# A hybrid RG-LRU and chunked attention layer: gates one step further behind, a bias table of distances in DRAM, and rearranged background loads

## The chip, the core and the metric

One core of a Trainium2 chip runs the whole kernel in one launch. The metric is the device time in microseconds (us) of one execution; the profile is one further execution, taken with the hardware profiler.

## What is computed

One layer of a streaming encoder, for 2048 prompt tokens and 32 sample tokens. Cut to what matters here:

```python
z = rms_norm(x, norm_g) @ w_in                 # 1024 -> 6 x 512
xl, gl, q, k, v, ga = split(z)
xc = b + sum(full[:, k:k + T] * w[k] for k in range(4))      # causal conv of xl
r = sigmoid(block_diag(xc, wa) + ba); i = sigmoid(block_diag(xc, wx) + bx)
log_a = -8 * r * softplus(-lam); a = exp(log_a)
u = sqrt(-expm1(2 * log_a)) * (i * xc)
h = scan(h[t] = a[t] * h[t-1] + u[t])                        # RG-LRU
s = q @ k.T / 8 + table[clip(distance, -256, 256)]           # per head, 64 + 512 frames
att = softmax(s) @ v
mix = concat([h * silu(gl), att * silu(ga)]) @ w_out
y = x + mix, then + (p @ w_pe) * sigmoid(rms_norm(y) @ w_pg)
```

The sample reads cached keys and values of 512 frames besides its own. Outputs are y for prompt and sample, the newest keys and values, and the last convolution rows and LRU states.

## The kernel before

Every matrix product is made of fp16 halves: each operand is split into a high and a low part, and three matmuls (high by high, high by low, low by high) stand for one (`products`, L177 to 185). The parts need a power-of-two scale, which comes from a maximum over the whole tensor; `all_max` (L81 to 91) takes it across partitions with a diagonal, one small matmul into a PSUM bank of its own (`psm`) and a reduction.

The prompt is 16 tiles of 128 tokens. `load_x` and `prep_x` (L214 to 236) load a tile, normalise and split it and transpose it by DMA into xT. `proj(i, b)` (L268) makes 24 matmuls of 512 columns for tile i and one of the four attention blocks of w_in (q, k, v, gate), and the `post_*` functions spill the result to DRAM. The w_in blocks are loaded and split at the start (`load_w_in`, `prep_w_in`, L243 to 264), through staging tiles of eight slots.

The LRU works in 8 chunks of 256 tokens, four blocks g of 128 channels each. `l_proj` (L537) makes 48 matmuls into a `psx` bank, ACT copies both halves out (the gate half z as it is), the conv is one POOL and three DVE instructions, and `l_split` makes X. `l_gates` (L593) makes four matmuls of X into the only `psg` bank; ACT takes two sigmoids each of r and of i (`th`) from it, POOL multiplies by i. `l_tail` (L612) works on all four blocks together: Tanh, two Exp, Sqrt and the sigmoid of z on ACT, then the scans and a product. `l_halves` spills the result. `l_steps` (L653) hands these out, with the gates one block behind.

The main loop (c = 2 to 5, from L762) takes eight steps a chunk; each step makes one attention projection, parts of the LRU of the chunk before, and three steps of `background` (L350), a generator of side jobs: the cached keys' and values' bounds and halves, the bias of each of eight heads, and bounds and halves of the output weights. For the bias, a 511-column row of each head's table, stored in DRAM (`ext_d`, L695 to 699), is loaded skewed to 128 partitions (L418), scaled by POOL, widened by ACT, masked by two memsets and stored to `bias_d`; four loads bring it back at the start of the attention (L892). Chunks 6 and 7 run in a denser phase after the loop, then the attention and the output stage.

The tile framework orders each engine's instructions by a simulated timeline: an instruction that is ready may be placed far ahead of its place in the program, unless it stands under `issue_after`, and a tile's slot is taken when its first instruction is placed. DMAs of the kernel are issued from SP in order.

Of the kernel before, what the change touches and what calls it, by code (L numbers as in the profile page):

```python
# [13 lines left out]
OP = mybir.AluOpType  # L14
# [20 lines left out]
def hybrid_layer(  # L35
# [91 lines left out]
    bias_d = dp.tile([128, H, 640], F32, name="biasd")  # L127
# [75 lines left out]
    ps_g = pool("ps_g", bufs=1, space=PSUM, stack=esl)  # L203
    ps_m = pool("ps_m", bufs=1, space=PSUM, stack=esl)
# [146 lines left out]
    def background():  # L351
        def load(src):
            st = stg_tile()
            nc.sync.dma_start(st, src)
            return st
# [4 lines left out]
        def bound(src):  # L360
            m = sm.tile([128, 2], F32, tag="ckm", name="ckm")
            for j in range(2):
                with tc.issue_after(last_w.ins):
                    st = load(cache(src, j))
                yield
                absmax(m[:, j:j + 1], st)
            nc.vector.tensor_tensor(m[:, 0:1], m[:, 0:1], m[:, 1:2], op=OP.max)
            a = sm.tile([128, 1], F32, tag="cka", name="cka")
            for _ in range(4):
                yield  # L370
            all_max(a, m[:, 0:1], last_mm[0])
            return a

        m = yield from bound(cache_k)
        absmax(mgq, gk_b)
        nc.vector.scalar_tensor_tensor(m, mgq, 8.0, m, op0=OP.mult, op1=OP.max)
        floor2(mbS, m)
        nc.vector.reciprocal(sS, mbS)
        nc.vector.tensor_scalar(sS, sS, 2.0 ** 14, None, op0=OP.mult)
        nc.vector.tensor_scalar(gkS, gk_b, sS, None, op0=OP.mult)  # L380
        absmax(mgq, gq_b)
        floor2(mgq, mgq)
        nc.vector.tensor_scalar(ratS, mbS, 2.0 ** -28, iscP, op0=OP.mult, op1=OP.mult)
        nc.vector.tensor_tensor(ratS, ratS, mgq, op=OP.mult)
        nc.vector.reciprocal(mgq, mgq)
        nc.vector.tensor_scalar(gqS, gq_b, mgq, 0.5, op0=OP.mult, op1=OP.mult)
        for j in range(2):
            st = load(cache(cache_k, j))
            yield
            for d in range(2):  # L390
# [7 lines left out]
                yield  # L398
        m = yield from bound(cache_v)
        mbV, sV = c1("mbV"), c1("sV")  # L400
        nc.vector.tensor_copy(mbV, m)
        nc.vector.reciprocal(sV, mbV)
        nc.vector.tensor_scalar(sV, sV, 2.0 ** 14, None, op0=OP.mult)
        nc.vector.reciprocal(ratC, u_v)
        nc.vector.tensor_scalar(ratC, ratC, mbV, 2.0 ** -34, op0=OP.mult, op1=OP.mult)
        for j in range(2):
            st = load(cache(cache_v, j))
            yield
            for d in range(2):
                t = Tp("vTo", [128, 2, 512], F16, 2)  # L410
                split(t[:, 0], t[:, 1], st[:, d], sV)
                nc.sync.dma_start(kc_d[2 * j + d][:, 1], t.rearrange("p a b -> p (a b)"))
                yield


        for h in range(H):
            bq = stg_tile().rearrange("p a b -> p (a b)")[:, :384]
            nc.sync.dma_start(bq, bass.AP(tensor=ext_d.tensor, offset=ext_d.offset + 511 * h, ap=[[1, 128], [1, 384]]))  # L418
            yield
# [10 lines left out]

        jobs = [(u_out[n], None, 0, 1.0, block(w_out[0], wo_d[n], n)) for n in range(2)]
        jobs += [(u_pg[n], 1, PG, 2.0 ** -11, block(w_ple_gate[0], wg_d[n], n)) for n in range(2)]
        jobs.append((u_pe, None, 0, 0.5, [(w_ple_proj[0, :, n * 512:(n + 1) * 512], we_d[:, n], 0) for n in range(2)]))
        for u, gcol, gsrc, um, parts in jobs:
            a = sm.tile([128, 4], F32, tag="absT", name="absT")

            def get(src):
                return load(src.rearrange("(k p) n -> p k n", p=128))

            nxt = get(parts[0][0])  # L440
            for j in range(len(parts)):
                st = nxt
                nxt = get(parts[(j + 1) % len(parts)][0])
                yield
                junk = Tp("hlA", [128, D], BF16, 2)
                nc.scalar.activation(junk, st.rearrange("p a b -> p (a b)"), AF.Abs, accum_out=a[:, j:j + 1])
            for _ in range(4):
                yield
            ma = w_max(a[:, :len(parts)], last_mm[0])
            yield  # L450
            sg = w_factors(ma, gcol, gsrc, u, um)
            for j, (_, dst, k0) in enumerate(parts):
                st = nxt
                if j + 1 < len(parts):
                    nxt = get(parts[j + 1][0])
                yield
                for k in range(2):
                    hl = Tp("hlA", [128, 2, 512], F16, 2)
                    s = sg[:, k0 + k:k0 + k + 1] if gcol is not None else sg[:, 0:1]
                    split(hl[:, 0], hl[:, 1], st[:, k], s)  # L460
                    nc.sync.dma_start(dst[:, k], hl)
# [79 lines left out]
    def l_proj(c, g):  # L541
# [26 lines left out]
        nc.scalar.activation(z, pt[:, 1, :n], AF.Copy, scale=u_gl)  # L568
# [13 lines left out]
    def l_split(c, g):  # L582
        n = width(c)
        xc = C[c]["i4"][:, g, :n]
        X = TL("X", [128, 2, CW], F16, 3)
# [26 lines left out]
    def l_tail(c):  # L612
        n, t = width(c), C[c]
        r, u, th, z, sq = (t[k][:, :, :n] for k in ("r4", "i4", "th4", "sl4", "sq4"))
        nc.vector.tensor_tensor(r, r, bc4(cl, n), op=OP.mult)
        nc.scalar.activation(th, r, AF.Tanh, scale=-1.0)
        nc.scalar.activation(sq, r, AF.Exp, scale=2.0)
        nc.scalar.activation(r, r, AF.Exp)
        nc.vector.scalar_tensor_tensor(th, sq, 1.0, th, op0=OP.add, op1=OP.mult)
        nc.scalar.activation(th, th, AF.Sqrt)  # L620
        nc.scalar.activation(sq, z, AF.Sigmoid)
        nc.vector.tensor_tensor(th, th, u, op=OP.mult)
        nc.gpsimd.tensor_tensor(z, z, sq, op=OP.mult)
        for g in range(4):
            init = 0.0 if c == 0 else col[:, SLR + g:SLR + g + 1] if c == SAMPLE else hlast[g]
            h = t["i4"][:, g, :n]
            nc.vector.tensor_tensor_scan(h, t["r4"][:, g, :n], th[:, g], init, op0=OP.mult, op1=OP.add)  # L627
            if c != SAMPLE:
                hlast[g] = h[:, n - 1:n]
            if c in (SAMPLE, NCH - 1):  # L630
                o = (28 if c == SAMPLE else 12) + g
                nc.vector.tensor_copy(small[:, o:o + 1], h[:, n - 1:n])
        nc.vector.tensor_tensor(z, t["i4"][:, :, :n], z, op=OP.mult)
# [19 lines left out]
    def l_steps(c):  # L653

        for g in range(5):
# [3 lines left out]
            if g:  # L659
                l_gates(c, g - 1)  # L660
# [108 lines left out]
    for c in range(2, NCH - 2):  # L769
        steps = [(i, b) for i in (2 * c, 2 * c + 1) for b in (1, 0, 2, 3)]  # L770
        lp, ls = ls, l_steps(c - 1)
        for n, (i, b) in enumerate(steps):
# [6 lines left out]
            for _ in range(3):  # L779
                next(bg, None)  # L780
# [111 lines left out]
    for h in range(0, H, 2):  # L892
        nc.sync.dma_start(bias[:, h:h + 2], bias_d[:, h:h + 2])
# [8 lines left out]
    def s_bias(u):  # L902

        S = T("S", [128, 640], F32, 3, ch)
        for j in range(4):
            nc.sync.dma_start(S[j * NS:(j + 1) * NS, :512 + NS], bias_d[:NS, 2 * j + u, :512 + NS])
# [345 lines left out]
```

## Time and profile before

| | before |
|---|---|
| median of 3 runs | 1249.12 us (1247.4 to 1251.3) |
| the profiled execution, its own time | 1244.72 us |
| span of the profiled execution | 1243.0 us |
| mean granted clock of TensorE | 0.951 |
| DMA bytes moved | 215.36 MB |

PE is TensorE, PEld its weight loads, DVE VectorE, ACT ScalarE, POOL GpSimd, SP the engine that issues DMAs. Waits are given with what ended them: the engine and line that released the waiting instruction. Times in a timeline count from the start of the span. A clock of 1.00 is full speed.

### The profile page before, as it was taken

Reading aid. Unit: us, or ns where it says so; the run is one execution under the profiler, and the core shown is the slowest. Engines: PE = TensorE matmul, PEld = TensorE weight load, DVE = VectorE, ACT = ScalarE, POOL = GpSimd, SP = SyncE. Lnnn points to the kernel's source line nnn. Section 1 sums busy time; section 2 is a strip of 40 time slices with the busy share of each in tenths; the row PEclk is TensorE's granted clock in tenths of the full one; section 3 lists DMA queues with packets and bytes.
Section 4 is the critical chain, followed back from the end, with each engine's and each line's share of the span. In section 5 each row is a group of like instructions: output and inputs, shape, how many; then the busy total and the mean of one; then the engine's idle time right before and its main releaser. Section 6 shows DMA issues by size and latency. Waiting matters only on the chain.

```text
span 1243.0 us, 22344 instructions
## 1 busy us (share of the span) xinstructions
PE 1074.7 (86%) x8365; PEld 621.9 (50%) x8365; DVE 827.6 (67%) x1804; ACT 613.3 (49%) x1078; POOL 479.6 (39%) x543
## 2 busy tenths in 40 slices
PE   3799998868698879898895589999999999999895
PEld 1345664643454555575642345555555555555442
DVE  5897465635775867657646685677777767777544
ACT  6532656347355857265664344444444444444223
POOL 2885243544643547454421221322222222222211
PEclk9899999988899989898997789999999999999998
DMA  8795317567658468341597987899889999999830
GB/s 293 188 231 173 86 37 174 146 195 190 192 148 233 145 196 231 100 109 35 160 313 233 235 157 156 177 203 188 185 189 191 183 198 191 192 198 188 197 69 26
DMA packets 357068, 215.36 MB, mean 173 GB/s; under 512 B 296016, under 2 KB 299392, under 8 KB 356832
## 3 DMA queue, kind: packets, MB, share of 16 engines
q1 hardware_dynamic: 356528, 213.41, 71.4%
q8 instruction: 65, 1.06, 0.4%
q10 hardware_dynamic: 432, 0.54, 0.1%
q14 instruction: 43, 0.35, 0.1%
HBM read 97.30 MB, written 46.24 MB: 115 GB/s over the span
## 4 chain that ended last, share of the span: by engine, by line
PE 21%; DMA 10%; DVE 9%; issue 5%; ACT 4%; POOL 2%; SPq 1%; POOLq 0%; ACTq 0%; DVEq 0%
PE psu L184 8%; PE psg L184 7%; DMA PT<-Phl 6%; PE pss L933 2%; PE pso L988 2%; DVE Phl L966 2%; PE pse L184 2%; DVE S L944 2%; DMA hT<-hn 1%; ACT Phl L965 1%; POOL Phl L963 1%; ACT S L950 1%; DVE i L627 1%; DVE gt L1103 1%; DMA out_dram<-t 1%
## 5 line engine op out<-in xcount | busy, mean ns | idle before, releaser
L184 PE MATMUL psp<-wA,xT 128*128 128x512 f16 x1536 | 357.5, 391 | 26.6 <-DMA xT<-xn 7.9
L184 PEld LDWEIGHTS <-xT 128*128 128x128 f16 x1536 | 152.6, 100 | 225.7 <-issue 47.3
L950 ACT ACTIVATE S<-S,nb,s 128x640 f32<-128x640 f32 (+5 forms) x130 | 110.5, 850 | 214.6 <-DVE nb L947 208.7
L553 PE MATMUL psx<-xT,wl 128*128 128x256 f16 x1536 | 184.5, 281 | 0.5 <-DVE wl L164 0.5
L184 PE MATMUL psg<-g,hT 128*128 128x512 f16 x768 | 179.1, 381 | 2.9 <-DMA hT<-hn 2.8
L553 PEld LDWEIGHTS <-wl 128*128 128x128 f16 x1728 | 159.3, 100 | 33.0 <-issue 5.4
L966 DVE TENSOR_TENSOR Phl<-S,Phl 128x640 f16<-128x640 f32 (+4 forms) x126 | 97.9, 781 | 88.5 <-POOL Phl L963 51.5
L988 PE MATMUL pso<-kv,PT 128*128 128x64 f16 (+1 forms) x1704 | 116.6, 194 | 25.9 <-DMA PT<-Phl 13.2
L988 PEld LDWEIGHTS <-PT 128*128 128x128 f16 (+2 forms) x1800 | 109.4, 99 | 48.1 <-DMA PT<-Phl 16.9
L963 POOL TENSOR_SCALAR Phl<-S 128x640 f16<-128x640 f32 (+4 forms) x63 | 48.8, 774 | 205.0 <-ACT S L950 175.0
L933 PE MATMUL pss<-kv,qT 128*128 128x128 f16 (+2 forms) x1200 | 107.2, 222 | 10.4 <-DVE mx L944 8.3
L184 PEld LDWEIGHTS <-hT 128*128 128x128 f16 x768 | 71.2, 98 | 80.7 <-DMA hT<-hn 4.0
L933 PEld LDWEIGHTS <-qT 128*128 128x128 f16 (+1 forms) x1200 | 93.8, 99 | 33.3 <-issue 19.9
L944 DVE CUSTOM_DVE_ANT_0 S<-pss,bias 128x640 f32<-128x640 f32 (+4 forms) x128 | 92.9, 731 | 7.1 <-PE pss L933 7.0
L184 PE MATMUL psu<-o,AT 128*128 128x512 f16 x384 | 90.7, 387 | 1.1 <-DMA AT<-An 1.1
L184 PE MATMUL psu<-o,L 128*128 128x512 f16 x384 | 88.3, 379 | 0.0
L1104 POOL TENSOR_TENSOR gt<-gt,h 128x512 f32<-128x512 f32 x32 | 42.2, 1319 | 63.1 <-DVE gt L1103 54.0
L588 ACT ACTIVATE X<-i,sx 64x256 f16<-64x256 f32 x64 | 32.2, 504 | 67.5 <-DVE i L578 66.6
L578 DVE SCALAR_TENSOR_TENSOR i<-xl,col,i 128x256 f32<-128x256 f32 x96 | 52.1, 543 | 16.4 <-POOL i L575 14.7
L96 POOL TENSOR_TENSOR fh<-fh,pw 128x8 f32<-128x8 f32 (+1 forms) x34 | 61.1, 1797 | 2.0
L605 PE MATMUL psg<-X,gw 128*128 128x256 f16 (+1 forms) x72 | 18.4, 280 | 45.3 <-ACT th L609 29.8
L184 PEld LDWEIGHTS <-AT 128*128 128x128 f16 x384 | 36.3, 100 | 41.9 <-issue 3.3
(289 smaller groups left out, 1694.2 us busy)
## 6 DMA issues: line engine op xcount, KB each, us to landing
stw<-in_w_in_dram SPq DMA_DIRECT2D x20, 512.0 KB, 6.5
x<-in_x_prompt_dram SPq DMA_DIRECT2D x16, 512.0 KB, 4.5
stg<-in_w_out_dram SPq DMA_DIRECT2D x16, 512.0 KB, 5.7
stg<-in_w_ple_gate_dram SPq DMA_DIRECT2D x16, 512.0 KB, 4.9
qT<-qd SPq DMA_DIRECT2D x32, 256.0 KB, 5.4
kv<-kvd SPq DMA_DIRECT2D x16, 512.0 KB, 4.4
h<-in_x_prompt_dram SPq DMA_DIRECT2D x16, 512.0 KB, 4.6
out_dram<-gt SPq DMA_DIRECT2D x32, 256.0 KB, 2.4
```

Of the source, the lines that this page charges most:

```text
L96: nc.gpsimd.tensor_tensor(dst, dst, pw[:R, :n], op=OP.pow)
L184: m = nc.tensor.matmul(ps[:R], lhsT=l(a), rhs=r(e), start=first and j == 0, stop=last and j == 2)
L553: m = nc.tensor.matmul(o, lhsT=wl[j][:, k, a, g * 128:(g + 1) * 128], rhs=rhs, start=i == 0, stop=i == 23)
L578: nc.vector.scalar_tensor_tensor(xc, xl[:, k:k + n], col[:, CWT + 4 * k + g:CWT + 4 * k + g + 1], xc, op0=OP.mult, op1=OP.add)
L588: nc.scalar.activation(X[q, o, :n], xc[q], AF.Copy, scale=sx[q, g:g + 1])
L933: last_mm[0] = nc.tensor.matmul(ps[rw, c], lhsT=q[:, h % 2, a * 4 + h // 2, :R], rhs=k[:, h, :n], start=a == 0, stop=a == 1)
L944: nc.vector.tensor_tensor_reduce(out=S[:, c0:c0 + W], in0=ps[:, c0:c0 + W], in1=bias[:, h, 640 - W:], op0=OP.add, op1=OP.max, scale=1.0, s ...
L950: nc.scalar.activation(S[:, c0:c0 + W], S[:, c0:c0 + W], AF.Exp, bias=nb[:, j:j + 1], scale=scP, accum_out=sums[i][:, e:e + 1])
L963: nc.gpsimd.tensor_scalar(v[:, 0, :W], P[:, :W], 1.0, 1.0, op0=OP.mult, op1=OP.mult)
L966: nc.vector.tensor_tensor(v[:, 1, :W], P[:, :W], v[:, 0, :W], op=OP.subtract)
L988: nc.tensor.matmul(o[rw, o0:o0 + HD], lhsT=t[:n, a * (WP // 128) + c0 // 128 + j, rw], rhs=v[:n, e, h * HD:h * HD + HD], start=first and m ...
L1104: (nc.vector if end else nc.gpsimd).tensor_tensor(gt[:R], gt[:R], s["h"][:R, c], op=OP.add)
```

## The change

- `all_max` puts its matmul into `ps_g`, which has two banks now; `ps_m` is gone.
- `l_steps` issues the gates two blocks behind for chunks 0 to 5 and the sample, one for chunks 6 and 7; X has four buffers, r4 and the gates' i two each.
- `l_proj` takes the sigmoid of z on ACT from PSUM and multiplies by z on DVE; the same two steps leave `l_tail`. The second Exp of `l_tail` runs in two halves.
- The last state of a chunk is copied to a small tile.
- `background` is a list of items. Loads are kept two ahead; weight halves are made one per step. The eight bias jobs are gone. In their place one DMA stores each head's 767-column row 128 times to `ext_d`, and the attention's four bias loads read that with a row step of 766, followed by two memsets each. The sample's bias is read the same way.
- `vTo` has one buffer. The main loop takes four background steps instead of three at every third step.

```diff
@@ all_max
-        ps = ps_m.tile([128, 128], F32, tag="m", name="psm")
+        ps = ps_g.tile([128, 2, CW], F32, tag="g", name="psm").rearrange("p a b -> p (a b)")[:, :128]
...
-    ps_g = pool("ps_g", bufs=1, space=PSUM, stack=esl)
-    ps_m = pool("ps_m", bufs=1, space=PSUM, stack=esl)
+    ps_g = pool("ps_g", bufs=2, space=PSUM, stack=esl)
@@ post_v
-        t = Tp("vTo", [128, 2, 512], F16, 2)
+        t = Tp("vTo", [128, 2, 512], F16, 1)
@@ background
-        for h in range(H):
-            bq = stg_tile().rearrange("p a b -> p (a b)")[:, :384]
-            nc.sync.dma_start(bq, bass.AP(tensor=ext_d.tensor, offset=ext_d.offset + 511 * h, ap=[[1, 128], [1, 384]]))
-            yield
-            b = stg_tile().rearrange("p a b -> p (a b)")[:, :640]
-            nc.gpsimd.tensor_scalar(b[:, 256:], bq[:, ::-1], iscP, 1.0, op0=OP.mult, op1=OP.mult)
-            nc.scalar.activation(b[:, 0:256], b[:, 256:257].to_broadcast([128, 256]), AF.Copy)
-            nc.gpsimd.memset(b[0:64, 576:640], -1e30)
-            nc.gpsimd.memset(b[64:128, 0:64], -1e30)
-            nc.sync.dma_start(bias_d[:, h], b)
...
+        def ext_load(_):
+            st8["ext"] = Tp("hlA", [128, D], BF16, 2).bitcast(F32)[:H, :384]
+            nc.sync.dma_start(st8["ext"], rel_bias[:, 129:513])
+
+        def ext_store(_):
+
+            e = stg_tile().rearrange("p a b -> p (a b)")[:H, :767]
+            nc.vector.tensor_scalar(e[:, 383:767], st8["ext"][:, ::-1], iscP[:H], None, op0=OP.mult)
+            nc.vector.tensor_copy(e[:, 0:383], e[:, 383:384].to_broadcast([H, 383]))
+            nc.sync.dma_start(ext_d, e.unsqueeze(1).to_broadcast([H, 128, 767]))
+
+        pause = [(None, ())] * 4
+        items = [(None, (ext_load,))] + pause + [(None, (ext_store,))]
+        for src, factors, half in ((cache_k, k_factors, k_half), (cache_v, v_factors, v_half)):
+            items += [(cache(src, j), (part_max(j),)) for j in range(2)] + pause
+            items += [(None, (cache_max, factors))]
+            items += [(cache(src, j), (half(j, 0), half(j, 1))) for j in range(2)]
...
+        todo, ready = [n for n, (src, _) in enumerate(items) if src is not None], {}
+        for n, (src, fs) in enumerate(items):
+            while todo and len(ready) < 2:
+                m = todo.pop(0)
+                ready[m] = stg_tile()
+                with tc.issue_after(last_w.ins) if m < 2 else nullcontext():
+                    nc.sync.dma_start(ready[m], items[m][0])
+            st = ready.pop(n, None)
+            for f in fs or (None,):
                 yield
...
+                if f is not None:
+                    f(st)
@@ l_proj
-        nc.scalar.activation(z, pt[:, 1, :n], AF.Copy, scale=u_gl)
+        zs = TL("zs", [128, CW])[:, :n]
+        nc.scalar.activation(zs, pt[:, 1, :n], AF.Sigmoid, scale=u_gl)
+        nc.vector.scalar_tensor_tensor(z, pt[:, 1, :n], u_gl, zs, op0=OP.mult, op1=OP.mult)
@@ l_gates
-            for k in ("r4", "th4", "sq4"):
-                C[c][k] = TL(k + b, [128, 4, n if b else CW])
-        r, xc, i = (C[c][k][:, g, :n] for k in ("r4", "i4", "th4"))
+            C[c]["r4"] = TL("r4" + b, [128, 4, n if b else CW], F32, 1 if b else 2)
+        r, xc = (C[c][k][:, g, :n] for k in ("r4", "i4"))
+        i = TL("ig", [128, CW], F32, 2)[:, :n]
@@ l_tail
-        nc.scalar.activation(sq, r, AF.Exp, scale=2.0)
+        for g in (0, 2):
+            sq = TL("sq2", [128, 2, CW])[:, :, :n]
+            nc.scalar.activation(sq, r[:, g:g + 2], AF.Exp, scale=2.0)
+            nc.vector.scalar_tensor_tensor(th[:, g:g + 2], sq, 1.0, th[:, g:g + 2], op0=OP.add, op1=OP.mult)
         nc.scalar.activation(r, r, AF.Exp)
-        nc.vector.scalar_tensor_tensor(th, sq, 1.0, th, op0=OP.add, op1=OP.mult)
         nc.scalar.activation(th, th, AF.Sqrt)
-        nc.scalar.activation(sq, z, AF.Sigmoid)
         nc.vector.tensor_tensor(th, th, u, op=OP.mult)
-        nc.gpsimd.tensor_tensor(z, z, sq, op=OP.mult)
@@ l_steps
-        for g in range(5):
+        late = 1 if c >= NCH - 2 else 2
+        for g in range(4 + late):
             if g < 4:
                 l_proj(c, g)
             yield
-            if g:
-                l_gates(c, g - 1)
+            if g >= late:
+                l_gates(c, g - late)
             yield
@@ start
-    ext = T("stw", [128, 2, 512], F32, 8, st0).rearrange("p a b -> p (a b)")[:H, :511]
-    nc.sync.dma_start(ext[:, 0:384], rel_bias[:, 129:513])
-    nc.vector.tensor_copy(ext[:, 384:511], ext[:, 383:384].to_broadcast([H, 127]))
-    ext_d = dp.tile([H, 511], F32, name="ext_d")
-    nc.sync.dma_start(ext_d, ext)
+    ext_d = dp.tile([H, 128, 767], F32, name="ext_d")
+
+    def bias_rows(h, R, W, n=1):
+
+        ap = [[766, R], [128 * 767, n], [1, W]] if n > 1 else [[766, R], [1, W]]
+        return bass.AP(tensor=ext_d.tensor, offset=ext_d.offset + 128 * 767 * h + 127, ap=ap)
@@ main loop
-            for _ in range(3):
+            for _ in range(4 if n % 3 == 0 else 3):
                 next(bg, None)
@@ attention
-        nc.sync.dma_start(bias[:, h:h + 2], bias_d[:, h:h + 2])
+        nc.sync.dma_start(bias[:, h:h + 2], bias_rows(h, 128, 640, 2))
+
+        nc.gpsimd.memset(bias[0:64, h:h + 2, 576:640], -1e30)
+        nc.gpsimd.memset(bias[64:128, h:h + 2, 0:64], -1e30)
```

## Rows read from the trace of the kernel before

**Rows 1.** The page, busy time of each engine over the whole span.

```profile
PE 1074.7 (86%) x8365; PEld 621.9 (50%) x8365; DVE 827.6 (67%) x1804; ACT 613.3 (49%) x1078; POOL 479.6 (39%) x543
```

**Rows 2.** Stretches: length, busy time of each engine, granted clock, DMA share, GB/s.

```profile
100.00:150.00 50.00, 49.74 (x316) 30.61 (x315) 31.72 (x64) 23.53 (x43) 20.35 (x23) 1.00 0.37 104
...
250.00:300.00 50.00, 34.53 (x186) 17.84 (x184) 19.31 (x40) 28.53 (x54) 20.24 (x37) 0.86 0.76 203
300.00:350.00 50.00, 38.93 (x331) 21.98 (x330) 38.82 (x68) 24.43 (x42) 32.00 (x27) 0.86 0.64 178
```

**Rows 3.** PE's waits, 190 to 450 us: us in total, times, longest.

```profile
PE psg L605 <- ACT th L609: 28.3, 7, 7.3
PE psp L182 <- DVE vTo L324: 5.2, 1, 5.2
PE psg L605 <- DVE X L589: 4.8, 1, 4.8
PE psp L184 <- DVE t L190: 4.8, 1, 4.8
```

**Rows 4.** PE's timeline from 245 us: start, us, operation, [idle before, releaser].

```profile
245.05 5.40 PE L553 MATMUL psx<-xT,wl 128*128 128x256 f16 x48
...
262.92 0.37 PE L605 MATMUL psg<-X,gw 128*128 128x256 f16 x1 [7.29 <-ACT th L609]
...
263.83 7.34 PE L553 MATMUL psx<-xT,wl 128*128 128x256 f16 x48
...
290.84 0.37 PE L605 MATMUL psg<-X,gw 128*128 128x256 f16 x1 [5.47 <-ACT th L609]
```

**Rows 5.** Groups of instructions, 180 to 660 us: busy, mean ns, idle before.

```profile
L578 DVE SCALAR_TENSOR_TENSOR i<-xl,col,i 128x256 f32<-128x256 f32 x78 | 42.5, 544 | 13.7 <-POOL i L575 12.4
L623 POOL TENSOR_TENSOR sl<-sl,sq 128x1024 f32<-128x1024 f32 x7 | 18.1, 2584 | 23.9 <-ACT sq L621 23.9
...
L421 POOL TENSOR_SCALAR stg<-stg,s 128x384 f32<-128x384 f32 x8 | 4.9, 616 | 12.5 <-DMA stg<-ext_d 8.5 <-DMA biasd<-stg 2.5 <-DVE hist L571 1.5
```

**Rows 6.** DMA issues: count, KB each, median us to landing.

```profile
bias<-biasd SPq DMA_DIRECT2D x4, 640.0 KB, 8.3
```

**Rows 7.** PE's timeline at the start and at the first scores.

```profile
35.77 5.90 PE L184 MATMUL psp<-wA,xT 128*128 128x512 f16 x19 [7.95 <-DMA xT<-xn]
...
41.56 5.13 PE L184 MATMUL psp<-wA,xT 128*128 128x512 f16 x23
...
650.42 0.39 PE L933 MATMUL pss<-kv,qT 128*128 128x128 f16 x4
```

**Rows 8.** SP's timeline at the start and before the attention: start, us to issue.

```profile
2.67 2.35 SPq L247 DMA_DIRECT2D stw<-in_w_in_dram  x4
12.08 1.43 SPq L236 DMA_TRANSPOSE xT<-xn  x1
13.62 1.22 SPq L218 DMA_DIRECT2D x<-in_x_prompt_dram  x1
...
21.23 0.35 SPq L696 DMA_DIRECT2D stw<-in_rel_bias_dram  x1
...
26.56 7.03 SPq L236 DMA_TRANSPOSE xT<-xn  x1
...
627.21 0.48 SPq L893 DMA_DIRECT2D bias<-biasd  x1
```

**Rows 9.** DMA queue q1, 1198.3 to 1198.9, then 1236.85 to 1237.45: packets, MB, share.

```profile
q1 hardware_dynamic: 99, 0.20, 90.1%
...
q1 hardware_dynamic: 48, 0.07, 47.9%
```

**Rows 10.** DVE's timeline at the start.

```profile
8.31 0.15 DVE L709 TENSOR_SCALAR s<-s 128x1 f32<-128x1 f32 x1
...
30.21 0.69 DVE L697 COPY stw<-stw 8x127 f32<-8x127 f32 x1 [0.16 <-DMA stw<-in_rel_bias_dram]
...
46.48 0.15 DVE L404 RECIPROCAL e<-u 128x1 f32<-128x1 f32 x1
```

More of the change, by code (lines that the diff above doesn't have):

```diff
@@ L126, in hybrid_layer @@
     kc_d = [dp.tile([128, 2, 1024], F16, name=f"kcd{j}") for j in range(4)]
-    bias_d = dp.tile([128, H, 640], F32, name="biasd")
     att_s = dp.tile([NS, 512], F32, name="attds")
@@ L351, in background, with first @@
     def background():
[L352 to L355, printed above, removed]
+        st8 = {}
         def cache(src, j):
             return src[0, 0, j * 256:(j + 1) * 256].rearrange("(t p) h d -> p t (h d)", p=128)
[L360 to L364, printed above, removed]
-                yield
-                absmax(m[:, j:j + 1], st)
+        def first(n):
+            st8["m"] = sm.tile([128, n], F32, tag=f"bgm{n}", name="bgm")
@@ L367, in bound, with part_max, f, cache_max @@
+        def part_max(j):
+            def f(st):
+                if j == 0:
+                    first(2)
+                absmax(st8["m"][:, j:j + 1], st)
+            return f
+        def cache_max(_):
+            m = st8["m"]
             nc.vector.tensor_tensor(m[:, 0:1], m[:, 0:1], m[:, 1:2], op=OP.max)
-            a = sm.tile([128, 1], F32, tag="cka", name="cka")
-            for _ in range(4):
-                yield
+            a = st8["a"] = sm.tile([128, 1], F32, tag="cka", name="cka")
@@ L371, in bound @@
             all_max(a, m[:, 0:1], last_mm[0])
[L372 to L390, printed above, removed]
+        def k_factors(_):
+            m = st8["a"]
+            absmax(mgq, gk_b)
+            nc.vector.scalar_tensor_tensor(m, mgq, 8.0, m, op0=OP.mult, op1=OP.max)
+            floor2(mbS, m)
+            nc.vector.reciprocal(sS, mbS)
+            nc.vector.tensor_scalar(sS, sS, 2.0 ** 14, None, op0=OP.mult)
+            nc.vector.tensor_scalar(gkS, gk_b, sS, None, op0=OP.mult)
+            absmax(mgq, gq_b)
+            floor2(mgq, mgq)
+            nc.vector.tensor_scalar(ratS, mbS, 2.0 ** -28, iscP, op0=OP.mult, op1=OP.mult)
+            nc.vector.tensor_tensor(ratS, ratS, mgq, op=OP.mult)
+            nc.vector.reciprocal(mgq, mgq)
+            nc.vector.tensor_scalar(gqS, gq_b, mgq, 0.5, op0=OP.mult, op1=OP.mult)
@@ L391, in background, with k_half, f @@
+        def k_half(j, d):
+            def f(st):
                 src = st[:, d].rearrange("p (h d) -> p h d", h=H)
@@ L397, in background, with v_factors @@
                 nc.sync.dma_start(kc_d[2 * j + d][:, 0], t.rearrange("p a b -> p (a b)"))
-                yield
-        m = yield from bound(cache_v)
+            return f
         mbV, sV = c1("mbV"), c1("sV")
[L401 to L410, printed above, removed]
+        def v_factors(_):
+            nc.vector.tensor_copy(mbV, st8["a"])
+            nc.vector.reciprocal(sV, mbV)
+            nc.vector.tensor_scalar(sV, sV, 2.0 ** 14, None, op0=OP.mult)
+            nc.vector.reciprocal(ratC, u_v)
+            nc.vector.tensor_scalar(ratC, ratC, mbV, 2.0 ** -34, op0=OP.mult, op1=OP.mult)
@@ L411, in background, with v_half, f @@
+        def v_half(j, d):
+            def f(st):
+                t = Tp("vTo", [128, 2, 512], F16, 1)
                 split(t[:, 0], t[:, 1], st[:, d], sV)
                 nc.sync.dma_start(kc_d[2 * j + d][:, 1], t.rearrange("p a b -> p (a b)"))
-                yield
-        for h in range(H):
-            bq = stg_tile().rearrange("p a b -> p (a b)")[:, :384]
-            nc.sync.dma_start(bq, bass.AP(tensor=ext_d.tensor, offset=ext_d.offset + 511 * h, ap=[[1, 128], [1, 384]]))
-            yield
-            b = stg_tile().rearrange("p a b -> p (a b)")[:, :640]
-            nc.gpsimd.tensor_scalar(b[:, 256:], bq[:, ::-1], iscP, 1.0, op0=OP.mult, op1=OP.mult)
-            nc.scalar.activation(b[:, 0:256], b[:, 256:257].to_broadcast([128, 256]), AF.Copy)
-            nc.gpsimd.memset(b[0:64, 576:640], -1e30)
-            nc.gpsimd.memset(b[64:128, 0:64], -1e30)
-            nc.sync.dma_start(bias_d[:, h], b)
+            return f
@@ new lines, in w_part, with f, w_bound, w_scale @@
+        def w_part(j):
+            def f(st):
+                if j == 0:
+                    first(4)
+                junk = Tp("hlA", [128, D], BF16, 2)
+                nc.scalar.activation(junk, st.rearrange("p a b -> p (a b)"), AF.Abs, accum_out=st8["m"][:, j:j + 1])
+            return f
+        def w_bound(n):
+            def f(_):
+                st8["a"] = w_max(st8["m"][:, :n], last_mm[0])
+            return f
+        def w_scale(u, gcol, gsrc, um):
+            def f(_):
+                st8["sg"] = w_factors(st8["a"], gcol, gsrc, u, um)
+            return f
@@ L427, in block, with w_half, f @@
+        def w_half(dst, k0, k, gcol):
+            def f(st):
+                sg = st8["sg"]
+                hl = Tp("hlA", [128, 2, 512], F16, 2)
+                s = sg[:, k0 + k:k0 + k + 1] if gcol is not None else sg[:, 0:1]
+                split(hl[:, 0], hl[:, 1], st[:, k], s)
+                nc.sync.dma_start(dst[:, k], hl)
+            return f
         def block(src, dst, n):
@@ L434, in background @@
         for u, gcol, gsrc, um, parts in jobs:
[L435 to L443, printed above, removed]
-                yield
[L445 to L461, printed above, removed]
+            srcs = [src.rearrange("(k p) n -> p k n", p=128) for src, _, _ in parts]
+            items += [(src, (w_part(j),)) for j, src in enumerate(srcs)] + pause
+            items += [(None, (w_bound(len(parts)), w_scale(u, gcol, gsrc, um)))]
+            items += [(srcs[j], [w_half(dst, k0, k, gcol) for k in range(2)]) for j, (_, dst, k0) in enumerate(parts)]
+        todo, ready = [n for n, (src, _) in enumerate(items) if src is not None], {}
[7 more added lines that the diff above has]
+            for f in fs or (None,):
+                yield
+                if f is not None:
+                    f(st)
     lt = []
@@ L584, in l_split @@
         xc = C[c]["i4"][:, g, :n]
-        X = TL("X", [128, 2, CW], F16, 3)
+        X = TL("Xs", [128, 2, NS], F16, 4) if c == SAMPLE else TL("X", [128, 2, CW], F16, 4)
         for o in range(2):
@@ L632, in l_tail @@
                 nc.vector.tensor_copy(small[:, o:o + 1], h[:, n - 1:n])
+        if c != SAMPLE:
+            hlast[0] = sm.tile([128, 4], F32, tag="hlast", name="hlast")
+            nc.vector.tensor_copy(hlast[0], t["i4"][:, :, n - 1])
         nc.vector.tensor_tensor(z, t["i4"][:, :, :n], z, op=OP.mult)
@@ L905, in s_bias @@
         for j in range(4):
-            nc.sync.dma_start(S[j * NS:(j + 1) * NS, :512 + NS], bias_d[:NS, 2 * j + u, :512 + NS])
+            nc.sync.dma_start(S[j * NS:(j + 1) * NS, :512 + NS], bias_rows(2 * j + u, NS, 512 + NS))
         return S
```

7 lines of the change are left out of this document (3 added, 4 removed).

## The prediction

> **What bounds the kernel now.** I read the page's busy table first: PE works 1074.7 of 1243.0 us [rows 1], so the end moves mostly when PE's idle time does, or its clock. The table of stretches shows where it is idle in the part that the change edits: from 100 to 150 us PE is busy 49.74 of 50 us at a granted clock of 1.00, but from 250 to 300 us only 34.53 at 0.86, and 38.93 in the next 50 us [rows 2]. The waits of PE between 190 and 450 us then name what it stood for: 28.3 us in seven waits of the gates' matmul (L605) for the ACT sigmoid of the block before (L609), 4.8 us for the split X (L589), and 5.2 and 4.8 us of projections behind late DVE instructions [rows 3]. PE's timeline shows how one such wait comes about: at 262.92 the gates' matmul has waited 7.29 us, and the 48 matmuls behind it take 7.34 us, where the same 48 took 5.40 us at 245.05 [rows 4]. The single psg bank holds a block's gates until ACT has read them, and PE works in order, so whatever is late on ACT or DVE stops it there.
>
> The profiled execution took 1244.72 us (span 1243.0), 4.4 us under the median of 1249.12. I sum changes on that execution and add them to the median.
>
> **Gates further behind, second psg bank.** Removed: 28.3 + 4.8 = 33.1 us of waits [rows 3]. With late=2 the gates' matmul comes one projection step (some 10 us by the spacing of rows 4) after the sigmoid that it used to follow, and with two banks it waits for the gates two blocks back. The slowed groups behind the waits come on top: 7.34 − 5.40 = 1.94 us for one; a share of that for each of eight waits is at most some 8 us. Upper end 41 us. The all_max matmul moves into the same two banks; it and the gates now share them, and the waits for its inputs (DVE) are not touched.
> What stays: the projections' 5.2 + 4.8 = 10 us behind DVE [rows 3].
>
> **Silu of the gate in l_proj.** POOL loses seven multiplications of 2.58 us [rows 5], ACT seven sigmoids over 1024 columns for 28 over 256; ACT keeps its three table loads a chunk, since gates and gate silu use one function. DVE gains one scalar_tensor_tensor over 256 columns per block. L578 is the same form: 0.544 us [rows 5], times 36 blocks is 19.6 us of DVE. In 250 to 350 us DVE is busy 58 of 100 us [rows 2], so there is room on average; but that instruction now frees the psx bank, and DVE is what those 10 us of projections already wait for. Lower end: all of it lands on the path, 33.1 − 19.6 = 13.5 us, less the waits of ACT's second Exp round for DVE (sq2 has one buffer, some 0.3 us in each of 8 chunks by half of L578's time): about 11 us.
>
> **Bias jobs out of the loop.** Gone are eight loads, eight POOL scalings of 0.616 us [rows 5], ACT copies, memsets and stores, with their place at 250 to 290 us. The waits at 262.92 and 290.84 (7.29 + 5.47 = 12.8 us [rows 4]) stand among them: POOL waited 12.5 us there, mostly for those loads [rows 5], and ACT and POOL stood in order behind. These 12.8 us lie inside the 33.1 and are not added again, but they go for two reasons, so they are the surest part. Gain taken: 27 us, two thirds of the way from 11 to 33.1, plus little for the clock.
>
> **Loads two ahead, halves one by one, vTo with one buffer.** The same loads and splits in another order; a stg tile is awaited less. I put it at nothing, cover being the DMA share of 0.76 and 0.64 between 250 and 350 us [rows 2]; the vTo buffer shared by post_v and the cache can cost one store's landing each time, again on a queue that the 5.2 us for vTo [rows 3] shows as tight. Plus or minus 5 us.
>
> **Bias at the start of attention.** Four loads now read skewed rows of 2.5 KB. Before, the loads of the same 640 KB landed 8.3 us after issue [rows 6], the first scores ran at 650.42 [rows 7], and the last load was issued at 627.21 [rows 8]: 15 us of cover beyond the landing. The eight memsets are small beside it. So nothing, and at double the landing time still nothing.
>
> **The table's store.** This is the new operation without a row. ext_store writes 8 × 128 × 767 × 4 = 3.14 MB to DRAM in one DMA out of eight partitions, 128 times the same 3 KB each. Two rows bound it. The store of a y tile from 128 partitions moved 0.20 MB in 0.6 us with the 16 engines 90.1% busy [rows 9], 0.20 / (16 × 0.6 × 0.901) = 23 GB/s an engine. At that pace eight engines, one a row of heads, take 3.14 / (8 × 0.0234) = 16.8 us, 16 engines 8.4. The sample's y store from 32 partitions moved its 32 rows of 2 KB (0.0656 MB) with 0.479 × 16 × 0.6 = 4.6 us of engine time [rows 9]: 14 GB/s an engine, 228 GB/s over all 16, 7.1 GB/s a partition. If what is reached scales with partitions, eight give 57 GB/s and the store takes 55 us. I take 55 us: among rows it is the one from few partitions with more than one packet an engine, and the fall from 23 to 14 GB/s shows that a narrow store is not the engines' own pace.
> [...]
>
> When it is issued decides the cost. ext_load and ext_store carry no issue_after, and instructions of the background already run far ahead of their place: its reciprocal L404 ran at 46.48 [rows 10], among the first projections. iscP, which the store's scaling reads, was ready after 8.31 us [rows 10]; SP stood free from 5.0 to 12.08 [rows 8]. So I expect the 12 KB load in that gap and the store at about 13.5 us, ahead of x(1) at 13.62 and of the weight loads behind it; and a later DMA waits behind earlier ones: the 12 KB of rel_bias, issued at 21.23 [rows 8], were what DVE had waited for when it copied them at 30.21 [rows 10]. So what follows on the held engines waits until about 68.5 us. What queues there: x tile 1, the transposition xT(1) issued at 26.56 and the w_in loads [rows 8]. The projection that started at 35.77 waited 7.95 us for just that xT [rows 7]; with landing it goes to some 74 us, 38 us later. Were the next block's weights late too, the projection of 41.56 [rows 7] would go to 90: 49 us. If it is issued late, at about 100 us, the stretch 100 to 150 has (1 − 0.37) × 50 = 31 us of free DMA [rows 2]; then 55 − 31 = 24 us are felt, since xT, qTo, kTo and the spill stores have few buffers. So 24 to 49 us, taken 38.
>
> **Sum.** 1249.1 − 27 + 38 = 1260 us (span 1254). Own range of this case: −33 + 24 gives 1240, −11 + 49 gives 1287.
>
> **Rivals.**
> (1) The store is short: eight engines at full pace, 16.8 us. Then, issued at 13.5, it holds them to some 30 us; PE's first 36 us are spent waiting for weights and xT anyway [rows 7], and 3 to 12 us are felt, 8 taken: 1249.1 − 27 + 8 = 1230 us, at best 1249.1 − 33 + 3 = 1219, at worst 1246. For it: nothing in this trace shows a DMA that reads one row many times, and the sample's rows are two packets an engine, a start more than a stream. Against it: the 32-partition store [rows 9]. The other side of the forecast.
> [...]
> (2) The store is long and the gates' gain does not come, because DVE, with 19.6 us more work, takes ACT's place as what PE waits for; PE then shows waits of psx for z instead of psg for th. Gain 8: 1249 − 8 + 38 = 1279 us.
> (3) The change doesn't do what it says: gates wait as long elsewhere, the store is short or hidden: 1249 − 10 + 8 = 1247 us.
> The forecast turns from slower to faster where the store's hold costs less than the gates give back, 27 us.
>
> **Numbers.** Forecast 0.45, rival 1 0.33, rival 2 0.12, rival 3 0.10. A measurement of this kernel can tell about 0.3% (3.7 us) from no change. Faster by more: rival 1 nearly whole (0.31), the early end of the forecast (0.06), some of rival 3 (0.03): 0.40. Within: 0.14, from the forecast's lower half with a late store and rival 3. Slower: 0.46. The range reaches from rival 1's middle, 1225, to past rival 2, 1281; outside lie the best of rival 1 and the worst of the forecast, some 0.15. Beside it stands the likeliest case's own 1240 to 1287.
>
> **What would show it.** Store: one issue on SP of 3 MB in the first 20 us, its landing after 40 to 60 us, PE idle before its second projection until 70 us or so; landing in under 20 us makes the forecast wrong and rival 1 right. Gates: PE's waits psg for ACT th between 190 and 450 under 5 us instead of 28.3; the slices from 250 to 350 us at 45 of 50 or more. Rival 2: psx or psp waits for DVE above 30 us there. Bias: no wait of the scores for it. The gain is misjudged if the waits go but the busy time of PE in those 300 us of stretch stays under 45 per 50.

## The result and the profile after

The changed kernel takes 1278.82 us (median of 6 runs, 1274.97 to 1283.94) against 1249.03 us (6 runs): ratio 1.0251, 95% interval 1.0225 to 1.0278, so 31 us slower. The forecast was 11 us slower. The profiled execution has a span of 1276.1 us where before had 1243.0; PE works as long as before [rows 1], so all of it is time in which PE stands.

The page's busy table of the changed kernel:

```profile
PE 1075.9 (84%) x8365; PEld 622.2 (49%) x8365; DVE 821.6 (64%) x1858; ACT 610.1 (48%) x1074; POOL 455.3 (36%) x518
```

The table of stretches of the changed kernel, columns as in [rows 2]:

```profile
100.00:150.00 50.00, 10.61 (x64) 6.07 (x63) 1.34 (x6) 0.60 (x1) 3.00 (x3) 0.66 0.94 56
150.00:200.00 50.00, 35.40 (x225) 22.65 (x225) 26.94 (x53) 15.21 (x28) 12.41 (x15) 0.80 0.44 109
250.00:300.00 50.00, 49.53 (x302) 29.26 (x301) 34.85 (x69) 30.74 (x51) 21.86 (x24) 1.00 0.62 147
300.00:350.00 50.00, 37.12 (x227) 20.24 (x227) 30.91 (x66) 26.27 (x51) 24.37 (x28) 0.91 0.81 220
```

From 100 to 150 us PE had been busy 49.74 us [rows 2]; now 10.61, with every other engine all but idle and the DMAs moving 56 GB/s at a busy share of 0.94. From 250 to 300 us PE is busier; how much of that is only the same work coming later is not shown.

PE's waits of the changed kernel, first 0 to 190 us, then 190 to 450 us, columns as in [rows 3]:

```profile
PE psp L183 <- DVE vTo L322: 54.0, 1, 54.0
PE psm L90 <- DVE dg L87: 22.4, 4, 11.1
...
PE psm L90 <- ACT ig L631: 8.3, 2, 7.8
PE psg L627 <- ACT ig L631: 6.6, 1, 6.6
PE psp L181 <- DVE t L291: 4.9, 1, 4.9
PE psp L181 <- DVE vTo L322: 4.2, 1, 4.2
```

One wait of 54.0 us is new. In the loop, psg waited 28.3 us for the gates' ACT before [rows 3]; now psg waits 6.6 us and the maxima's matmul, in the same banks, 8.3. SP's timeline of the changed kernel shows what stood there:

```profile
86.16 0.70 SPq L446 DMA_DIRECT2D hlA<-in_rel_bias_dram  x1
...
94.89 0.83 SPq L453 DMA_DIRECT2D ext_d<-stg  x1
97.58 22.29 SPq L302 DMA_DIRECT2D kvd<-kTo  x1
119.92 4.74 SPq L327 DMA_DIRECT2D kvd<-vTo  x1
124.76 18.30 SPq L315 DMA_TRANSPOSE qTo<-qN  x1
161.87 0.40 SPq L476 DMA_DIRECT2D stg<-in_cache_k_dram  x1
```

The table's store was issued at 94.89. The next DMA, the spill of kTo, took 22.29 us to issue alone, and SP issued three DMAs in the 64 us until 161.87. The changed kernel's DMA view from 100 to 160 us (busy share of the engines in tenths and GB/s, each in 40 slices; then KB and microseconds to landing):

```profile
DMA  4444444444444754564494444444444444444445
GB/s 49 51 49 49 49 51 49 49 51 49 49 49 49 132 58 49 87 100 49 51 93 49 49 51 49 51 49 49 49 49 51 49 49 49 51 49 49 49 49 65
...
kvd<-kTo SPq DMA_DIRECT2D x1, 256.0 KB, 64.9
kvd<-vTo SPq DMA_DIRECT2D x1, 256.0 KB, 43.2
```

The store runs at 49 GB/s from start to end, with the engines under half busy in most slices: its packets run for 63 us, from 98.3 to 161.5. (Of the share of 0.94 in the table, 0.48 are the store's packets and 0.45 those of the transposition behind it, which take up to 32 us each.) The spill behind it lands after 64.9 us. With one vTo buffer, post_v of the next tile waits for the spill of the one before; its projection's bank stays taken, and PE stands. The wait of ACT that shows this link, and then PE's timeline of the changed kernel on both sides of the hole:

```profile
ACT vTo L321 <- DMA kvd<-vTo: 60.2, 1, 60.2
```

```profile
107.50 3.11 PE L573 MATMUL psx<-xT,wl 128*128 128x256 f16 x27
164.60 8.06 PE L183 MATMUL psp<-wA,xT 128*128 128x512 f16 x24 [53.99 <-DVE vTo L322]
```

The slow store with two vTo buffers was not run, so how much of the wait the second buffer would have saved is open.

### The profile page after: what moved, and what is told of

It is laid out like the page before. It is cut to its first block, busy times and chain, and to the rows that moved or that the text cites. A ratio compares the mean times of both kernels' runs of the same rounds, so it can differ in the third digit from the quotient of the medians.

```text
span 1276.1 us, 22345 instructions
## 1 busy us (share of the span) xinstructions
PE 1075.9 (84%) x8365; PEld 622.2 (49%) x8365; DVE 821.6 (64%) x1858; ACT 610.1 (48%) x1074; POOL 455.3 (36%) x518
## 4 chain that ended last, share of the span: by engine, by line
PE 23%; DMA 12%; DVE 11%; ACT 9%; issue 7%; POOL 5%; SPq 1%; POOLq 0%; ACTq 0%; DVEq 0%
PE psu L183 8%; PE psg L183 7%; DMA PT<-Phl 4%; PE pss L963 3%; PE pso L1018 2%; PE pse L183 2%; DVE Phl L996 2%; DVE S L974 1%; DVE i L600 1%; DMA hT<-hn 1%; POOL fh L96 1%; DMA kvd<-vTo 1%; ACT Phl L995 1%; DMA wgd<-hlA 1%; ACT X L610 1%
## 5 line engine op out<-in xcount | busy, mean ns | idle before, releaser
L183 PE MATMUL psp<-wA,xT 128*128 128x512 f16 x1536 | 362.6, 395 | 73.2 <-DVE vTo L322 54.0
L573 PE MATMUL psx<-xT,wl 128*128 128x256 f16 x1536 | 178.3, 276 | 0.0
L95 POOL TENSOR_SCALAR fh<-ssqh,e 128x8 f32<-128x8 f32 (+1 forms) x34 | 19.6, 578 | 105.1 <-DVE ssqh L282 75.9
```

The lines of the kernel that those rows point to most:

```text
L183: m = nc.tensor.matmul(ps[:R], lhsT=l(a), rhs=r(e), start=first and j == 0, stop=last and j == 2)
L573: m = nc.tensor.matmul(o, lhsT=wl[j][:, k, a, g * 128:(g + 1) * 128], rhs=rhs, start=i == 0, stop=i == 23)
```

## The experiments

Every ratio is to the kernel before in the same set of runs, with its 95% interval. Where two kernels of different sets are compared, it is by these ratios.

**1. The same store from 128 partitions (e1_wide).**

```diff
-            st8["ext"] = Tp("hlA", [128, D], BF16, 2).bitcast(F32)[:H, :384]
-            nc.sync.dma_start(st8["ext"], rel_bias[:, 129:513])
+            st8["ext"] = Tp("hlA", [128, D], BF16, 2).bitcast(F32)[:, :384]
+            for h in range(H):
+                nc.sync.dma_start(st8["ext"][h * 16:h * 16 + 16], rel_bias[h:h + 1, 129:513].to_broadcast([16, 384]))
...
-            nc.sync.dma_start(ext_d, e.unsqueeze(1).to_broadcast([H, 128, 767]))
+            nc.sync.dma_start(ext_d.rearrange("h (r j) n -> (h r) j n", j=8), e.unsqueeze(1).to_broadcast([128, 8, 767]))
```

> The changed kernel with one part altered: each head's row is loaded into 16 partitions, so that the same 3.14 MB leave from 128 partitions, eight copies each. Theory (the store from eight partitions holds the DMA queue for 63 us and nearly all of the loss is PE's wait behind it): the store takes 8 to 12 us, PE's 54 us wait for vTo goes to under 5, and the time falls by 50 to 58 us to 1221 to 1229, under the kernel before. Rival A (the store only collides with something else that is late there, the cached keys' jobs or the single vTo buffer): a wait for vTo or psm of over 20 us stays between 95 and 165 us and the time stays over 1245.

Measured: 1230.13 us, ratio 0.9885 (0.9847 to 0.9923). The DMA view of this kernel from 98 to 108 us, GB/s in slices, and then its table of stretches:

```profile
GB/s 393 426 413 405 409 430 405 442 417 417 393 417 356 368 319 270 356 282 344 319 307 344 307 344 295 123 356 380 393 442 393 417 389 393 381 294 305 297 267 174
```

```profile
100.00:150.00 50.00, 49.35 (x320) 31.02 (x318) 31.29 (x66) 18.49 (x35) 16.55 (x20) 1.00 0.56 159
```

The store is done in 11 us, in a stretch in which the DMAs move some 350 GB/s, PE is busy 49.35 of 50 us there, and the 54 us wait is gone. From 1.0251 to 0.9885 is 0.0366, 46 us: the store's hold, and it alone turns a faster kernel into a slower one. Rival A falls. The time is a little above the 1221 to 1229 expected.

**2. The same eight rows in partitions 0, 4, ... 28 (e2_spread).** Where the change has `[:H]` for the two tiles, this has `[:4 * H]`, and the load and the store use `[0:4 * H:4]`; a memset clears the first tile.

```diff
-            nc.sync.dma_start(ext_d, e.unsqueeze(1).to_broadcast([H, 128, 767]))
+            nc.sync.dma_start(ext_d, e[0:4 * H:4].unsqueeze(1).to_broadcast([H, 128, 767]))
```

> The changed kernel with the same eight rows in partitions 0, 4, 8 to 28 instead of 0 to 7; the store's bytes, its packets of 3068 bytes and its eight outermost rows are the same. [...] Rival B (each partition gives 6 to 7 GB/s, whichever it is): packets of 470 ns as before, 63 us, time 1275 to 1283. Rival C (eight engines of 16 are the limit): no change either, as the number of outermost rows is the same; B and C are then told apart by the packet's duration.

Measured: 1232.48 us, ratio 0.9909 (0.9874 to 0.9945). The DMA view from 97 to 113 us of this kernel, GB/s in slices:

```profile
GB/s 215 199 199 207 207 199 184 184 238 192 184 184 184 230 310 379 207 292 430 212 184 201 297 259 206 184 184 230 192 184 184 192 222 192 192 184 222 199 184 192
```

Still eight partitions and eight outermost rows, but 184 to 200 GB/s instead of 49, some 23 GB/s a row, which is the pace of one engine in the 128-partition store [rows 9]. So neither the number of partitions nor that of the rows set the 49 GB/s; their place did, and rivals B and C fall. What makes the one place slower than the other, no run shows.

**3. One small store, then DRAM to DRAM (e3_d2d).** The 24 KB go to a small table, and one DMA copies that 128 times, with the 128 outermost.

```diff
+            nc.sync.dma_start(ext_1, e)
+            nc.sync.dma_start(ext_d.rearrange("h r n -> r h n"), bass.AP(tensor=ext_1.tensor, offset=ext_1.offset, ap=[[0, 128], [767, H], [1, 767]]))
```

> The changed kernel with the table made in two steps: 24 KB from the eight partitions to DRAM once, and one DMA from there to the 128 copies in DRAM, with the 128 outermost. Theory (the source in SBUF is what is slow, not the writing of 3.14 MB): 16 engines, the second DMA takes 10 to 20 us, time 1222 to 1240. Rival (writing 3 KB rows to DRAM many times is slow whatever the source): 40 us and more, time over 1255.

Measured, one run: 1231.48 us. The copy's row among the DMA issues of this kernel:

```profile
ext_d<-ext SPq DMA_DIRECT2D x1, 3068.0 KB, 15.0
```

15.0 us to landing for the same writes, where the store from partitions 0 to 7 ran for 63 us: reading those partitions, not writing 1024 rows of 3 KB, was slow.

**4. The slow store at the start (e4_early).** Load, scaling and store stand behind iscP in the startup, in staging tiles.

> The changed kernel with the load and the store of the table at the start, in staging tiles, and not in the background; store from eight partitions as in the change. This is the case that the prediction took for the likeliest, at its price of 38 us (24 to 49). Theory: the hold is 63 us wherever the store stands, and at the start PE waits for loads that queue behind it, 40 to 60 us: time 1262 to 1285. Rival (early it falls into time in which PE waits for weights and transpositions anyway): 25 us or less, time 1235 to 1250.

Measured: 1276.35 us, ratio 1.0258 (1.0223 to 1.0292), the same as the change. SP's timeline of this kernel, and then PE's:

```profile
31.57 0.85 SPq L742 DMA_DIRECT2D ext_d<-stw  x1
32.52 62.62 SPq L245 DMA_DIRECT2D stw<-in_w_in_dram  x7
```

```profile
103.75 0.26 PE L90 MATMUL psm<-dg,ones 128*128 128x128 bf16 x1 [54.44 <-DVE dg L87]
```

Weight loads take 62.62 us to issue, and PE waits 54.44 us for the maximum over them. In both places that were tried, the hold costs PE about 54 us.

**5 to 7. One part undone in the kernel of the first experiment.** e5_late1 has `late = 1` in every chunk. e6_banks_as_before has `ps_g` with one bank and `ps_m` with one. e7_silu_in_tail copies z in l_proj and has, in l_tail:

```diff
+        for g in (0, 2):
+            sq = TL("sq2", [128, 2, CW])[:, :, :n]
+            nc.scalar.activation(sq, z[:, g:g + 2], AF.Sigmoid)
+            nc.gpsimd.tensor_tensor(z[:, g:g + 2], z[:, g:g + 2], sq, op=OP.mult)
```

> The kernel of the first experiment (store from 128 partitions) with the gates one block behind in every chunk, as before; two shared banks stay. Theory (the step further behind is what takes PE's waits for the gates' sigmoid away): waits of psg for the gates' ACT of 10 us and more come back between 190 and 450 us, time 5 to 15 us above the first experiment's, ratio to the kernel before 0.993 to 1.001 against 0.9885. Rival (the second bank alone does it): ratio 0.985 to 0.991.

> The kernel of the first experiment with the banks as before: one for the gates, one for the maxima's matmul; gates two blocks behind. There the profile of the first experiment shows psm waiting 14.6 us for the gates' ACT between 190 and 450 us, as both share the banks. Theory (sharing gives back about half of what the gates gain): psm's waits for ACT go, those of psg stay under 10 us since the gates come later, ratio 0.975 to 0.985. Rival (a single bank brings the gates' waits back, 28 us as before): ratio 0.990 to 1.000.

> The kernel of the first experiment with z copied by ACT in l_proj and its sigmoid and the product on POOL in l_tail, in two halves, as before the change in all but that. Theory (DVE's 36 instructions are hidden, and so was POOL's product): ratio within 0.004 of the first experiment's 0.9885. Rival 2 of the prediction (DVE's added 19.6 us land on the path): time falls by 8 to 20 us, ratio 0.972 to 0.982. Third possibility (the product on POOL held the tail up): ratio over 0.993.

Measured: 1236.37 us, ratio 0.9905 (0.9879 to 0.9932); 1241.50 us, 0.9937 (0.9911 to 0.9963); 1238.88 us, 0.9920 (0.9894 to 0.9946); all against 0.9885. Each undone part costs 2 to 7 us by the middle values, but every interval meets that of the first experiment, so no single part is clearly told apart from nothing. The theories of e5 and e6 fall, and so does rival 2 in e7. In e5, with two banks and the gates only one block behind, psg has no wait for the gates' ACT between 190 and 450 us; the lines of psg for X and of psm are

```profile
PE psg L628 <- DVE X L612: 8.5, 4, 4.7
PE psm L90 <- ACT ig L632: 7.7, 3, 4.3
```

So it is the second bank that takes the waits for ACT away, as e5's rival has it, and its ratio lies in the rival's range. The step further behind takes those for X: the first experiment's kernel has none of these there. Giving the maxima a bank of their own does not help when the gates have only one: PE's waits of e6, 190 to 450 and then 450 to 700 us, are

```profile
PE psg L629 <- ACT ig L633: 21.8, 7, 8.6
...
PE psg L629 <- ACT ig L633: 18.5, 5, 8.8
```

which is the 28.3 us of [rows 3] less 6.5, with the gates a step further behind. And e7 did not get faster with DVE relieved, so rival 2 of the prediction falls; its ratio lies within the 0.004 of its theory.

**8. The bias part alone in the kernel before (e8_bias_alone).** The eight jobs go, and the table of the first experiment takes their place, at the background's start.

> The kernel before with the bias part alone: table of 128 copies, stored from 128 partitions, read skewed at the attention; the eight bias jobs gone from the background; gates, banks, silu, loads as before. Theory (the bias jobs cause the waits at 262.92 and 290.84, 12.8 us, and those go with them): ratio 0.985 to 0.993. Rival (the gates' waits return elsewhere, and the change's gain is that of the gates): ratio 0.996 to 1.002.

Measured: 1250.32 us, ratio 1.0020 (1.0001 to 1.0040): no gain. Its profile shows that the loop got better and the start worse: PE's waits up to 190 us add up to 43.8 us against 33.2 before, and between 190 and 450 us to 42.9 against 47.3. PE's timelines of the start, of e8, then of e9 below, which has the start of before:

```profile
21.10 6.33 PE L183 MATMUL psp<-wA,xT 128*128 128x512 f16 x20 [0.20 <-DVE wA L163]
39.18 0.26 PE L90 MATMUL psm<-dg,ones 128*128 128x128 bf16 x1 [11.69 <-DVE dg L87]
```

```profile
27.89 0.22 PE L90 MATMUL psm<-dg,ones 128*128 128x128 bf16 x1
35.93 6.26 PE L183 MATMUL psp<-wA,xT 128*128 128x512 f16 x19 [7.82 <-DMA xT<-xn]
42.02 0.22 PE L90 MATMUL psm<-dg,ones 128*128 128x128 bf16 x1
```

The change took a 12 KB load, a small copy and a 16 KB store out of the startup. In the order of PE's instructions, the second block's maximum then stands ahead of the second projection instead of behind 19 of its matmuls, and PE, which works in order, stood for it. The changed kernel has the same order: its psm waits 11.08 us at 39.57.

**9. The start's lines put back in the first experiment's kernel (e9_old_start).**

```diff
+    ext_o = T("stw", [128, 2, 512], F32, 8, st0).rearrange("p a b -> p (a b)")[:H, :511]
+    nc.sync.dma_start(ext_o[:, 0:384], rel_bias[:, 129:513])
+    nc.vector.tensor_copy(ext_o[:, 384:511], ext_o[:, 383:384].to_broadcast([H, 127]))
+    ext_od = dp.tile([H, 511], F32, name="ext_od")
+    nc.sync.dma_start(ext_od, ext_o)
```

> The kernel of the first experiment with the four lines at the start put back that the change took out (the 12 KB load, the copy and the 16 KB store, to a table that nothing reads). In the built order of PE the second block's maximum then stands behind 19 matmuls of the second projection again, as before; without the lines it stands ahead of them, and the profile of the first experiment shows PE waiting 11.7 us for it at 39.14. Theory (the start's order costs the change some 5 to 10 us of its gain, though the lines look free): PE's waits to 190 us fall from 38.3 to 33 or less, time 4 to 9 us lower, ratio to the kernel before 0.981 to 0.985. Rival (the waits only shift, since weights and transpositions come when they come): ratio 0.987 to 0.990.

Measured: 1221.60 us, ratio 0.9822 (0.9799 to 0.9844), just under the first experiment's whole interval: 0.0063, 8 us, for lines whose result nobody reads. PE's waits up to 190 us fell from 38.3 to 34.5 us, not to 33, so the start itself shows only about half of the gain; the rest is not traced. This version beats the kernel before by 22 us and the change by 53 (by the ratios).

**10 to 12. The bias part with the old start; the maxima in psx; the rest without gates, banks and silu.** e10 is e8 with the same lines put back. e11 is e9 with the maxima's matmul in `ps_x`. e12 is e9 with the three parts of experiments 5 to 7 undone together.

> The kernel before with the bias part alone, as in the eighth run, and those four lines left at the start. Theory (the bias part does take 8 to 12 us out of the loop, and the start's new order hid that in the eighth run): waits to 190 us near 33 instead of 43.8, ratio 0.990 to 0.996. Rival (the bias part gives nothing): ratio 0.999 to 1.003.

> The kernel of e9 with the maxima's matmul in the three psx banks instead of the gates' two. Theory (sharing with the gates is a cost: psm waited 14.6 us for the gates' ACT in the first experiment): these waits go, and the time falls by 5 to 12 us against e9. Rival (psx is then held by a maximum whose diagonal is late, and the LRU's matmuls wait instead): time equal to e9 within 3 us, or higher.

> The kernel of e9 with the gates one block behind, the banks as before and the gate's silu in the tail: what is left of the change is the bias part, the rearranged background and the LRU's tiles. Theory (gates, banks and silu are worth 0.010 together, by the sum of runs five to seven): ratio 0.010 above e9's, near 0.993. Rival (the parts stand in for each other, so that less or more goes when all go): ratio within 0.004 of e9's, or over 1.000.

Measured: e10 1239.52 us, ratio 0.9974 (0.9957 to 0.9991), a gain of 3 us, between the two expectations. It is 0.0046, 6 us, under e8, with intervals apart: the start's lines are worth something here too, and PE's waits up to 190 us are 36.8 us against e8's 43.8. Between 190 and 450 us PE's waits add up to 46.4 us, against 47.3 before; psg's are

```profile
PE psg L603 <- ACT th L607: 15.8, 4, 8.9
PE psg L603 <- DVE X L587: 9.5, 2, 8.6
```

e11 1223.60 us, 0.9835 (0.9814 to 0.9857), no different from e9. e12 1229.46 us, 0.9892 (0.9867 to 0.9916), 0.0070 above e9 with intervals apart, less than the 0.010 of the sum. PE's waits between 190 and 450 us of e9, then of e11:

```profile
PE psm L90 <- ACT ig L632: 14.1, 3, 8.3
PE psg L628 <- ACT ig L632: 7.2, 1, 7.2
```

```profile
PE psp L183 <- DVE t L308: 12.8, 1, 12.8
PE psm L90 <- DVE dg L87: 6.2, 2, 3.1
PE psg L628 <- ACT ig L632: 4.1, 2, 2.9
```

In the psx banks the maxima no longer wait for the gates, 14.1 us, and a projection waits 12.8 us for DVE instead: the rival's equal time, by another wait than it named.

## Why the prediction was wrong

The direction and the long store were right; the size was not. The sum was −27 + 38 = +11 us. Measured against the first experiment, which has the change without the slow store, it is a gain of 14 us (0.9885) and a hold of 46 (1.0251 less 0.9885), which add up to the 31 measured by construction. Two terms failed: the gain, taken at 27, came out 13 us smaller, and the hold, taken at 38, came out 8 us larger. Both lie near the bad ends that the prediction gave them, 11 to 33 and 24 to 49. That the time lies between 1225 and 1281 all the same is luck: that upper end was there for rival 2, whose cause did not occur. By its steps:

- **The store's duration: right in kind.** 55 us from the 32-partition row [rows 9]; it ran at 49 GB/s for 63 us. Per partition the row gave 7.1 GB/s and the store had 6.2, but that scaling was luck: experiment 2 shows eight partitions at 23 GB/s each.
- **When it is issued: wrong.** The step said 13.5 us, by [rows 8, 10]; it was 94.89, as its 12 KB load was issued only at 86.16. That load writes to an hlA tile, one of two slots that the weight staging uses at the start; that this kept it back is argued, not shown.
- **What a late store costs: a step that failed.** "Then 55 − 31 = 24 us are felt", as 63% of the DMA engines' time was free in that stretch. That free share was no cover: the later DMAs landed only when the store did, the kTo spill 64.9 us after its issue and the vTo spill 43.2 us after its own. What covered was only what PE could still do without a new DMA, and that was 107.50 + 3.11 − 97.58 = 13 us from the first DMA that was held. The store's 63 us less that are 50, beside 54.0 us waited and 46 lost against a kernel whose store still takes some 10; early and late cost the same (experiment 4). The early case's price of 38 us, which went into the sum, stood on a store of 55 us and the wait for xT; in experiment 4 the weight loads behind the store took 62.62 us to issue and PE waited 54.44 us for the maximum over them, which the prediction had priced at 49. Measured there is 46 (1.0258 less 0.9885).
- **The gates' gain: the larger miss.** "Removed: 28.3 + 4.8 = 33.1 us of waits", taken at 27 with the bias. The waits of psg for the gates' ACT went from 28.3 to 6.6 us, near the forecast; by e5 the second bank did that. But 8.3 us came back in psm, as the maxima now wait for the gates' bank, which that step put aside ("the waits for its inputs (DVE) are not touched"), and with a short store psm's come to 14.1 (e9). Gates, banks and silu together are worth 9 us (0.9892 to 0.9822).
- **Bias out of the loop: over-sized as a part of its own.** "The surest part", 12.8 us, gave 3 us alone (experiment 10). The psg waits for ACT did fall by some 12 us, but those for X rose from 4.8 to 9.5, and PE's waits in the loop as a whole fell by 0.9. With the 9 us above, the term of 27 measured 12.
- **Loads two ahead, "put at nothing": wrong.** e12 holds the bias part, the new background and the LRU's tiles and is at 0.9892; the bias part alone is at 0.9974. The difference, 0.0082 or 10 us, is the background with its extra step and vTo's one buffer, the LRU's tiles and the halved steps of `l_tail`; which of them is open.
- **What the sum lacked.** The lines that left the start were counted as nothing; with them back the time is 8 us lower. That their order is the cause is shown for the wait at the start, some 4 us, and argued for the rest. So the gain of 14 us is 12 + 10 − 8, where the sum had 27; the parts were taken out in one order, and another might share the gain out differently.
- **Bias at the start of attention: right.** The four skewed loads landed after 5.5 to 9.6 us, and PE did not wait for them.
- **Rivals.** Rival 1's forecast, 1230 us with a short store, is what experiments 1 to 3 measured, 1230 to 1232; the store was not short as the change has it. Rival 2, at 1279, has the measured time but not its cause: DVE did not take the gates' place.

## What to carry to other kernels

Price a DMA that leaves from a few neighbouring partitions by a measured one of that kind (here 49 GB/s from eight), and as a hold for the DMAs behind it (here the two spills behind it landed after 64.9 and 43.2 us), not as bytes against a free share; spread the source over the partitions, here a few changed lines for 46 us. Waits that go are not yet time that goes: here psg's for ACT fell by 21.7 us in the loop, and gates, banks, silu and bias gave 12 in all. When a change removes instructions, compare the order of each engine's instructions before and after where they stood. And undo parts together as well as alone: the three that showed 2 to 7 us each alone, none clearly told apart from nothing, showed 9 us together, clear of the intervals.

## What the runs showed of the hardware that was not expected

Eight rows of 3 KB read 128 times gave 49 GB/s from partitions 0 to 7 and 184 to 200 GB/s from partitions 0, 4, ... 28. Behind the first, a 256 KB spill needed 22.29 us to be issued and 64.9 us to land while the DMAs moved mostly 49 GB/s, where some 350 were moved while the same bytes left from 128 partitions; in experiment 4 seven weight loads behind it needed 62.62 us to be issued.
